# Seven block products for the down-projection, with the activation sums made ahead of it and kept in DRAM

## The chip, the cores and the metric

The kernel runs on one core of a Trainium2 chip. The core has five engines that each follow their own list of instructions: TensorE (PE, matrix products, with a weight load, PEld, ahead of each), VectorE (DVE), ScalarE (ACT), GpSimd (POOL) and SyncE (SP), which here issues all transfers between DRAM and the on-chip memory. Results of TensorE land in eight accumulator banks of 128 x 512 floats. The metric is the device time of one execution in microseconds (us).

## The reference

The reference is a decoder block on 1024 tokens of width 1024, in float32: two attention branches, then a gated MLP with a causal convolution of width 3. Only the MLP matters here. `h` is the modulated norm of the residual stream `x`, `g_f` a row of 1024 numbers worked out from the conditioning vector, D_FF is 2816.

```python
u = h @ w_up                                              # 1024 x 5632
u = conv_b + sum(conv_w[j] * up[:, j:j + s] for j in range(3))
gate, val = u[..., :2816], u[..., 2816:]
x = x + g_f[:, None, :] * ((silu(gate) * val) @ w_down)   # the up stage, then the down stage
return rmsnorm(x, norm_final_g)
```

## The kernel before

Every float32 operand of a product is split into a high and a low part (`hi_act` on ACT writes the high one, `lo_dve` on DVE or `lo_pool` on POOL subtracts it to get the low one), and `mm3` (L95 to L97) issues three matmuls for one: high by high, high by low, low by high. One matmul multiplies a 128 x 128 block by 128 x 512 into one bank.

**The up stage** (`ffn_up`) runs over 22 blocks `j` of 128 hidden columns, tokens on the free axis (1024 of them, two halves of 512). For each block it makes the gate's and the value's columns by seven products instead of eight (a scheme of Strassen and Winograd: sums of blocks are multiplied, and the results are combined): `product` calls of four `mm3` each into the banks x1, x5, x6, x7, combined by ACT copies (`copied`, L1209), seeds (`seed`, L1180: a bank copied into another to go on accumulating there) and DVE subtractions (L1234, L1236). Then come the convolution (`conv`, L1194 on ACT, L1196 on DVE), Silu (L1245) and the product of both (L1247), which is the 128 x 1024 activation block `act`; L1248 stores it to DRAM as `dram_act`.

**The down stage** (`begin_down`, `ffn_down`) is a plain product: for each half of 512 output columns, 22 blocks `k` of the hidden axis by 8 token tiles, each an `mm3`: 2 x 22 x 8 x 3 = 1056 matmuls into the eight banks `mm`. For each block, SP loads `ahp_act` back, ACT and DVE split it (`split_act`: `ahp_ah`/`ahp_al`, in the second half also `an_ah`/`an_al`), and `scaled_rows` loads two blocks of `w_down`, multiplies them on POOL by the row `g_f` (L1124; `gf`) and splits them (`wd_wh`, `wd_wl`). `begin_down` starts this during the last block of the up stage. At the end of the first half DVE adds the eight banks to the residual (L1316), POOL multiplies by the final gain `gl` (L1326). In the second half each token tile is finished by itself: addition (L1333), sum of squares (L1284 on ACT), `rstd` (L102 to L107, small operations), ACT and DVE scale the two halves (L1338, L1339), and SP stores them.

The order on each engine's list is set by a scheduler when the kernel is built, not by the order of the code alone; tiles come from pools in which a new tile waits for the readers of the one that had its place. SP's list is one queue: a transfer that waits holds up all behind it.

## Time and profile before

| what | value |
|---|---|
| median of three runs (lowest, highest) | 1670.74 us (1667.92, 1671.0) |
| the profiled execution: its time, and its span in the trace | 1672.49 us, 1670.4 us |
| instructions | 21073, of them 7702 on PE |
| last matmul of the up stage starts | 1412.36 us |
| first, last matmul of the down stage start | 1418.44 us, 1661.54 us |

Times in the trace count from the span's start. A row of the timeline gives start, duration, engine, line, operation, output tile <- input tiles, shapes, the number of instructions in the row, and in brackets how long the engine was idle ahead of it and what released it. A matmul row's duration (0.39 us) is longer than the distance to the next start (0.23 us), since matmuls are pipelined. Names of tiles begin with their pool: `ps_` is an accumulator bank, `dn_`, `ahp_`, `wd_`, `uw_`, `wr_` are on chip, `dram_` and `in_` in DRAM.

### The profile page before, as it was taken

To read this page: it belongs to the slowest core of one execution; us is meant where nothing else is said; L and a number is where in the kernel's file an instruction comes from. 1 tells how busy PE (TensorE), PEld (TensorE's weight loads), DVE (VectorE), ACT (ScalarE), POOL (GpSimd) and SP (SyncE) were. 2 spreads that over 40 slices of the span, in tenths; PEclk is the share of its full clock that TensorE was granted. 3 is DMA by queue.
4 is the path that set the end of the run, shared out by engine and by line. 5 is a ranking of instruction groups with operands and counts; after the bars stand their busy time and mean duration, and the time that the engine had idled before them with its cause. 6 is when DMAs were issued, how large, how long until landed. Compare 5 with 4: busy or idle time off the path is not lost.

```text
span 1670.4 us, 21073 instructions
## 1 busy us (share of the span) xinstructions
PE 1587.7 (95%) x7702; PEld 1305.3 (78%) x7702; DVE 1048.6 (63%) x1662; ACT 778.2 (47%) x1355; POOL 432.5 (26%) x366
## 2 busy tenths in 40 slices
PE   7899989999979999999998969999999998999997
PEld 3788868888868888887877757888888886788886
DVE  5755666666555656666656698777677774435545
ACT  3424345555444555566433356555555554224324
POOL 1322035665761222202245320000000001324430
PEclk9999999999999999999999979999999999999999
DMA  8435497766564443427435323222222221844443
GB/s 286 139 102 180 166 259 190 211 171 200 148 169 108 113 124 99 123 65 244 138 118 202 125 64 102 84 91 78 88 76 76 81 90 64 291 143 150 164 151 114
DMA packets 172276, 233.33 MB, mean 140 GB/s; under 512 B 10786, under 2 KB 109794, under 8 KB 170830
## 3 DMA queue, kind: packets, MB, share of 16 engines
q1 hardware_dynamic: 172174, 232.01, 44.8%
q8 instruction: 60, 0.98, 0.2%
q14 instruction: 42, 0.34, 0.1%
HBM read 165.90 MB, written 53.48 MB: 131 GB/s over the span
## 4 chain that ended last, share of the span: by engine, by line
PE 46%; DVE 4%; DMA 2%; ACT 1%; issue 1%; POOL 1%; DVEq 0%; ACTq 0%; POOLq 0%; SPq 0%
PE ps_mm L95 11%; PE ps_mm L96 11%; PE ps_mm L97 11%; PE ps_sd L95 4%; PE ps_sd L96 4%; PE ps_sd L97 4%; POOL wr_wr L1124 1%; DMA wr_wr<-in_w_out_dram 1%; DMA wr_wr<-in_w_up_dram 1%; DVE up_u L1196 1%; DMA o_raw<-dram_o 0%; DVE wx_w L85 0%; PE ps_mm L1022 0%; PE psA_pt L97 0%; PE psA_pt L95 0%
## 5 line engine op out<-in xcount | busy, mean ns | idle before, releaser
L1124 POOL TENSOR_TENSOR wr_wr<-wr_wr,ahp_gf 128x512 f32<-128x512 f32 x22 | 33.8, 1560 | 481.9 <-DMA ahp_act<-dram_act 411.6
L95 PE MATMUL psA_fill<-hT_hi,ws_wh 128*128 128x512 f32 x352 | 150.0, 426 | 0.0
L750 ACT ACTIVATE att_p<-psA_s,small_soft 128x128 f32<-128x128 f32 (+7 forms) x128 | 95.0, 742 | 105.0 <-DVE small_soft L744 103.3
L88 POOL TENSOR_TENSOR ws_wl<-wr_wr,ws_wh 128x512 fp32r<-128x512 f32 x62 | 82.6, 1336 | 228.6 <-ACT ws_wh L76 205.7
L97 PE MATMUL psA_fill<-hT_hi,ws_wl 128*128 128x512 f32 x352 | 139.3, 396 | 0.0
L96 PE MATMUL psA_fill<-hT_lo,ws_wh 128*128 128x512 f32 x352 | 139.3, 396 | 0.0
L740 PE MATMUL psA_s<-opn_k,opn_q 96*128 96x256 f32 (+7 forms) x480 | 114.5, 358 | 17.2 <-DMA opn_k<-opn_stg 11.3
L744 DVE TENSOR_REDUCE small_soft<-psA_s 128x1 f32<-128x128 f32 (+7 forms) x128 | 96.1, 752 | 54.5 <-PE psA_s L742 53.9
L1196 DVE SCALAR_TENSOR_TENSOR up_u<-up_u,cw_cw,up_u 128x1023 f32<-128x1023 f32 x88 | 110.9, 1281 | 3.5 <-ACT up_u L1194 2.8
L95 PE MATMUL ps_mm<-wd_wh,ahp_ah 128*128 128x512 f32 x256 | 100.7, 393 | 6.8 <-ACT ahp_ah L76 6.8
L740 PEld LDWEIGHTS psA_s<-opn_k,opn_q 96*128 96x128 f32 (+1 forms) x480 | 81.8, 191 | 26.6 <-issue 16.6
L96 PE MATMUL ps_mm<-wd_wl,ahp_ah 128*128 128x512 f32 x256 | 100.4, 392 | 0.0
L97 PE MATMUL ps_mm<-wd_wh,ahp_al 128*128 128x512 f32 x256 | 99.8, 393 | 0.0
L85 DVE TENSOR_TENSOR ahp_al<-ahp_act,ahp_ah 128x1024 fp32r<-128x1024 f32 x32 | 42.0, 1317 | 88.0 <-ACT ahp_ah L76 88.0
L85 DVE TENSOR_TENSOR att_ptl<-psA_pt,att_pth 128x512 fp32r<-128x512 f32 x96 | 66.1, 688 | 33.9 <-ACT att_pth L76 33.5
L752 DVE TENSOR_SCALAR att_p<-att_p,small_soft 128x128 f32<-128x128 f32 (+7 forms) x128 | 84.1, 657 | 4.1
L769 PE MATMUL psA_pt<-const_ident,att_p 128*128 128x128 f32 x576 | 86.3, 272 | 0.0
L76 ACT ACTIVATE ahp_ah<-ahp_act 128x1024 fp32r<-128x1024 f32 x32 | 33.9, 1061 | 107.5 <-PE ps_mm L96 94.5
L97 PEld LDWEIGHTS psA_fill<-hT_hi,ws_wl 128*128 128x128 f32 x352 | 66.4, 189 | 15.7
L76 ACT ACTIVATE uw_sh<-uw_s 128x1024 fp32r<-128x1024 f32 x44 | 46.8, 1063 | 63.5 <-PE ps_mm L96 28.2
L95 PEld LDWEIGHTS psA_fill<-hT_hi,ws_wh 128*128 128x128 f32 x352 | 67.4, 191 | 9.6
L281 POOL TENSOR_TENSOR att_acc<-att_acc,att_lw 128x512 f32<-128x512 f32 x56 | 73.6, 1314 | 4.3
(411 smaller groups left out, 4518.9 us busy)
## 6 DMA issues: line engine op xcount, KB each, us to landing
wr_wr<-in_w_up_dram SPq DMA_DIRECT2D x46, 512.0 KB
ahp_act<-dram_act SPq DMA_DIRECT2D x44, 512.0 KB
att_lw<-in_w_ada_dram SPq DMA_DIRECT2D x64, 256.0 KB
wr_wr<-in_w_in_dram SPq DMA_DIRECT2D x28, 512.0 KB
dram_act<-up_u SPq DMA_DIRECT2D x22, 512.0 KB
wr_wr<-in_w_down_dram SPq DMA_DIRECT2D x22, 512.0 KB
ada_wada<-in_w_ada_dram SPq DMA_DIRECT2D x16, 512.0 KB
opn_v<-dram_v SPq DMA_DIRECT2D x16, 512.0 KB
```

Of the source, the lines that this page charges most:

```text
L76: self.nc.scalar.activation(out, in_, AF.Copy, scale=scale)
L85: self.nc.vector.tensor_tensor(out=out, in0=in_, in1=f32(hi), op=ALU.subtract)
L88: self.nc.gpsimd.tensor_tensor(out=out, in0=in_, in1=f32(hi), op=ALU.subtract)
L95: mm(ps, lhsT=lh, rhs=rh, start=start, stop=False, skip_group_check=onto)
L96: mm(ps, lhsT=lh, rhs=rl, start=False, stop=False, skip_group_check=onto)
L97: mm(ps, lhsT=ll, rhs=rh, start=False, stop=stop, skip_group_check=onto)
L740: mm(o, lhsT=l, rhs=r[:, keys], start=n_ == 0, stop=diag is None and n_ == len(passes) - 1)
L744: nc.vector.tensor_reduce(out=st[:, 0:1], in_=view(s), axis=AX.X if i < 4 else AX.XY, op=ALU.max, negate=True)
L750: nc.scalar.activation(po, view(s), AF.Exp, bias=st[:, 0:1], accum_out=st[:, 1:2])
L752: nc.vector.tensor_scalar(out=pr, in0=pr, scalar1=st[:, 2:3], scalar2=None, op0=ALU.mult)
L769: nc.tensor.transpose(pt[:, n * 256 + e * P : n * 256 + (e + 1) * P], pr[:, kb * P : (kb + 1) * P], self.ident)
L1196: nc.vector.scalar_tensor_tensor(out=dst[:, back:], in0=u[:, : S - back], scalar=cw[:, tap, jj : jj + 1], in1=dst[:, back:], op0=ALU.mult, ...
```

## The change

The down stage becomes a seven-product scheme too. Its matrices are cut in two by two: the hidden axis into even and odd blocks (11 pairs `m`), the tokens into two halves, the output columns into two halves. The 11 pairs are worked in seven entries, two of one pair, four of two, one of one. The left factors are A11, A12, A22 (parts of the activation) and four sums S1 to S4 of such parts; the right ones B11, B21, B22 (blocks of `w_down`) and sums N1, T2, N3, N4.

- **In the up stage**, `stored` writes the parts of `act` to DRAM, and at each odd block POOL makes the four sums (128 x 512 each), which are stored too: seven left factors of 11 blocks. The seed x7 is gone: the products N3 and N4 accumulate on in x6. The pool of sums holds two tiles of each kind in place of three.
- **`begin_down`** loads and splits the first two entries of A11 and B11 (pairs 10 and 9) during the last block, into places of the up stage's gate operands.
- **`ffn_down`** runs seven products of 11 blocks x 4 token tiles x 3 matmuls = 924 matmuls, and four matmuls that only open the banks Y: 928. For each step (a product and an entry) `operands` loads the left factor (`ring_ar`) and the right one (`ring_br`, or a sum kept on chip), and ACT and DVE split both, one step ahead. The sums N1, T2, N4 of `w_down` are made on DVE in products 0 and 1 and kept. Rows of the residual, `gf` and `gl` are loaded during product 0.
- `w_down` isn't multiplied by `g_f` any more; `result` multiplies the banks by it (L1375, L1379) before the residual is added (L1380). So 22 POOL multiplications per half go, and 40 DVE operations at the ends of products 1, 4, 5 and 6 come (in place of 16 additions).

```diff
@@ ffn_up @@
-            x7 = self.seed(x6, 1.0)
             t = copied(x6)
...
-            self.product(x7, s3, "N3", False)
-            V(out=uv[:, upper], in0=x7, in1=c5, op=ALU.subtract)
+            self.product(x6, s3, "N3", False)
+            V(out=uv[:, upper], in0=x6, in1=c5, op=ALU.subtract)
...
-            self.dma(self.d_act[j], act)
+            self.stored(j, act)
@@ stored @@
+        self.dma(self.place("A12", m), act[:, lower])
+        self.dma(self.place("A22", m), act[:, upper])
+        x, z = (self.upp([P, S], F32, "u", 7) for _ in range(2))
+        G(out=x[:, lower], in0=even[:, upper], in1=act[:, upper], op=ALU.add)
+        G(out=x[:, upper], in0=even[:, lower], in1=even[:, upper], op=ALU.add)
+        G(out=z[:, lower], in0=x[:, lower], in1=even[:, lower], op=ALU.add)
+        G(out=z[:, upper], in0=z[:, lower], in1=act[:, lower], op=ALU.add)
+        for n, y in (("S1", x[:, lower]), ("S3", x[:, upper]), ("S2", z[:, lower]), ("S4", z[:, upper])):
+            self.dma(self.place(n, m), y)
@@ ffn_down @@
-        for k in range(2, NJ):
-            if k % 2 == 0:
-                weights = self.scaled_rows(a["w_down"], k, ns, gain0, self.down_room)
-            held[k % 2] = split_act(self.ahp, k, 2), weights.pop(0)
-            for t in range(NT if k < NJ - 2 else 0):
-                product(acc, t, k, held[k % 2])
...
+        def result(acc, minus, x, ns):
+            if minus is None:
+                y = dn([P, 512], F32, "y", 2)
+                V(out=y, in0=acc, in1=gf[:, ns], op=ALU.mult)
+            else:
+                y = minus
+                V(out=y, in0=acc, in1=minus, op=ALU.subtract)
+                V(out=y, in0=y, in1=gf[:, ns], op=ALU.mult)
+            V(out=x[:, ns], in0=y, in1=x[:, ns], op=ALU.add)
...
+        products = [("A11", "B11", X), ("A12", "B21", X), ("S2", "T2", Y), ("S1", "N1", X), ("S3", "N3", Y), ("S4", "B22", X), ("A22", "N4", Y)]
...
+        for n, (p, i) in enumerate(steps):
+            held = ahead
+            if n + 1 < len(steps):
+                q, k = steps[n + 1]
+                ahead = operands(*products[q][:2], k)
+            matmuls(acc, held, i == 0, i == last, i in (0, last))
+            if (p, i) == (0, 3):
+                self.dma(gf, self.d_row.to_broadcast([P, D]))
+                self.dma(gl, a["norm_final_g"].rearrange("(o d) -> o d", o=1).to_broadcast([P, D]))
+                xs = rows(0)
...
+            elif p == 5:
+                for t in range(4):
+                    result(X[t], saved_t[t], xs[t], sides[1])
+                    finished(t, xs[t], sides[1], squares[t])
```

Three places of the lists, before and after. First SP, where the up stage ends. Before, the last activation block's store (`dram_act_77`) stands behind the loads of the first down blocks, which need earlier blocks alone:

```order
L73 DMA ahp_gf_12393<-dram_row_130 128x512
L73 DMA ahp_act_12409<-dram_act_56_139 128x1024
L73 DMA ahp_act_12415<-dram_act_57_140 128x1024
L73 DMA wr_wr_12587<-in_w_down_dram 128x2x512
L73 DMA dram_act_77_160<-up_u_12419 128x1024
L73 DMA ahp_act_12529<-dram_act_58_141 128x1024
L73 DMA ahp_act_12559<-dram_act_59_142 128x1024
```

Now the last pair's parts and sums (`dram_S_98` is S4) stand ahead of the first loads of the ring, the third entry's operands (`ring_ar_12586`, `ring_br_12588`) among them:

```order
L76 DMA dram_S_77_160<-up_u_12506 128x512
L76 DMA dram_S_84_167<-up_u_12507 128x512
L76 DMA dram_S_98_181<-up_u_12507 128x512
L76 DMA ring_br_12570<-in_w_down_dram 128x512
L76 DMA ring_br_12572<-in_w_down_dram 128x512
L76 DMA ring_br_12575<-in_w_down_dram 128x512
L76 DMA ring_br_12578<-in_w_down_dram 128x512
L76 DMA ring_ar_12586<-dram_A_58_141 128x1024
L76 DMA ring_br_12580<-in_w_down_dram 128x512
L76 DMA ring_br_12583<-in_w_down_dram 128x512
L76 DMA ring_br_12588<-in_w_down_dram 128x2x512
```

What moved: six transfers of `w_down` blocks for the sums and two operand loads now follow the last store, in one queue.

Second, SP in product 0, a new place. `ring_ar_12698` and `ring_br_12700` are the operands of the sixth entry (pairs 1, 2); `ring_br_12650` and `12653` are blocks for the sums of the entry before:

```order
L76 DMA ring_br_12650<-in_w_down_dram 128x2x512
L76 DMA ring_br_12653<-in_w_down_dram 128x2x512
L76 DMA dn_gl_12566<-in_norm_final_g_dram 128x1024
L76 DMA dn_x_12690<-dram_x_48_131 128x1024
L76 DMA dn_x_12692<-dram_x_49_132 128x1024
L76 DMA dn_x_12694<-dram_x_50_133 128x1024
L76 DMA dn_x_12696<-dram_x_51_134 128x1024
L76 DMA ring_ar_12698<-dram_A_61_144 128x1024
L76 DMA ring_br_12700<-in_w_down_dram 128x2x512
```

Nine transfers of 512 KB stand in a row here, of which the first two wait for a place in the ring.

Third, DVE where results are taken. Before, at the end of the first half, one addition per bank:

```order
L85 TENSOR_TENSOR an_al_13203<-ahp_act_13204,an_ah_13202 128x1024
L1316 TENSOR_TENSOR dn_x_1_12439<-ps_mm_1_12449,dn_x_1_12439 128x512
L1316 TENSOR_TENSOR dn_x_2_12440<-ps_mm_2_12450,dn_x_2_12440 128x512
L1316 TENSOR_TENSOR dn_x_3_12441<-ps_mm_3_12451,dn_x_3_12441 128x512
L1316 TENSOR_TENSOR dn_x_4_12442<-ps_mm_4_12452,dn_x_4_12442 128x512
L1316 TENSOR_TENSOR dn_x_5_12443<-ps_mm_5_12453,dn_x_5_12443 128x512
L85 TENSOR_TENSOR an_al_13209<-ahp_act_13210,an_ah_13208 128x1024
```

Now, at the end of product 5, twelve operations for four banks and eight small ones stand between the low parts of the first entry of product 6 (`ring_al_13949`, `ring_bl_13953`) and those of its second (`ring_al_14043`, `ring_bl_14047`). The first rows, and the last:

```order
L88 TENSOR_TENSOR ring_al_13949<-ring_ar_13946,ring_ah_13948 128x512
L88 TENSOR_TENSOR ring_bl_13953<-dn_N_5_12569,ring_bh_13952 128x512
L1378 TENSOR_TENSOR dn_t_13261<-ps_x_1_12522,dn_t_13261 128x512
L1378 TENSOR_TENSOR dn_t_13263<-ps_x_2_12523,dn_t_13263 128x512
L1379 TENSOR_TENSOR dn_t_13261<-dn_t_13261,dn_gf_12565 128x512
L1379 TENSOR_TENSOR dn_t_13263<-dn_t_13263,dn_gf_12565 128x512
L1380 TENSOR_TENSOR dn_x_12690<-dn_t_13261,dn_x_12690 128x512
L1380 TENSOR_TENSOR dn_x_12692<-dn_t_13263,dn_x_12692 128x512
```

```order
L1380 TENSOR_TENSOR dn_x_12696<-dn_t_13267,dn_x_12696 128x512
L108 TENSOR_TENSOR small_rstd_13975<-small_rstd_13975 128x1
L108 TENSOR_TENSOR small_rstd_13993<-small_rstd_13993 128x1
L88 TENSOR_TENSOR ring_al_14043<-ring_ar_14040,ring_ah_14042 128x512
L109 SCALAR_TENSOR_TENSOR small_rstd_13975<-small_rstd_13975 128x1
L109 SCALAR_TENSOR_TENSOR small_rstd_13993<-small_rstd_13993 128x1
L88 TENSOR_TENSOR ring_bl_14047<-dn_N_5_12569,ring_bh_14046 128x512
```

What moved: the split of the next operands follows the whole of the results. At the ends of products 1 and 4 the pattern is the same, with 8 and 12 operations and no small ones between.

## Rows read from the trace of the kernel before

**Rows 1.** The page, first lines: the span, and PE's busy time, share and instructions.

```profile
span 1670.4 us, 21073 instructions
PE 1587.7 (95%) x7702; PEld 1305.3 (78%) x7702; DVE 1048.6 (63%) x1662; ACT 778.2 (47%) x1355; POOL 432.5 (26%) x366
```

**Rows 2.** Windows: PE, PEld, DVE, ACT, POOL busy, granted clock, DMA share, GB/s.

```profile
1010.00:1412.70 402.70, 402.41 (x1750) 328.07 (x1748) 289.54 (x310) 217.38 (x269) 5.02 (x4) 1.00 0.26 83
1412.70:1418.40 5.70, 0.04 (x1) 0.00 (x0) 5.63 (x6) 5.42 (x8) 0.00 (x0) 0.76 0.00 0
1418.40:1662.00 243.60, 242.36 (x1056) 198.98 (x1056) 118.19 (x145) 83.44 (x127) 77.16 (x48) 0.99 0.49 168
1662.00:1670.40 8.40, 0.00 (x0) 0.00 (x0) 3.81 (x15) 2.51 (x7) 0.00 (x0) 0.67 0.44 163
```

**Rows 3.** Waits of PE, 1395 to 1671: total, times, longest.

```profile
PE ps_mm L95 <- ACT ahp_ah L76: 6.8, 2, 5.7
```

**Rows 4.** Timeline of PE: five matmuls of the up and down stages.

```profile
1412.36 0.39 PE L97 MATMUL ps_sd<-t_N,uw_vl 128*128 128x512 f32 x1
1418.44 0.79 PE L95 MATMUL ps_mm<-wd_wh,ahp_ah 128*128 128x512 f32 x1 [5.70 <-ACT ahp_ah L76]
...
1424.03 0.40 PE L95 MATMUL ps_mm<-wd_wh,ahp_ah 128*128 128x512 f32 x1
...
1441.94 0.39 PE L96 MATMUL ps_mm<-wd_wl,ahp_ah 128*128 128x512 f32 x1
...
1661.54 0.39 PE L97 MATMUL ps_mm<-wd_wh,an_al 128*128 128x512 f32 x1
```

**Rows 5.** Windows behind three idle times of PE (3.5, 5.7 and 1.1 us).

```profile
932.10:935.00 2.90, 2.89 (x11) 2.71 (x12) 2.44 (x4) 2.40 (x6) 1.58 (x2) 0.50 0.37 125
1418.40:1422.50 4.10, 4.06 (x9) 2.87 (x10) 4.10 (x6) 1.46 (x2) 0.00 (x0) 0.50 0.66 218
1443.70:1446.00 2.30, 2.30 (x10) 1.92 (x11) 2.23 (x2) 1.06 (x1) 0.78 (x1) 1.00 0.35 121
```

**Rows 6.** Timeline of DVE and POOL around the end of the up stage.

```profile
1404.68 5.02 POOL L1124 TENSOR_TENSOR wr_wr<-wr_wr,ahp_gf 128x512 f32<-128x512 f32 x4 [411.57 <-DMA ahp_act<-dram_act]
1412.18 5.12 DVE L1196 SCALAR_TENSOR_TENSOR up_u<-up_u,cw_cw,up_u 128x1023 f32<-128x1023 f32 x4 [1.38 <-ACT up_u L1194]
1418.42 1.22 DVE L1247 TENSOR_TENSOR up_u<-up_u,up_u 128x1024 f32<-128x1024 f32 x1
```

**Rows 7.** Transfers: a window of the down stage, two loads' issue, the user of the second.

```profile
1430.00:1436.00 6.00, 6.00 (x28) 4.99 (x27) 3.52 (x4) 1.94 (x3) 0.00 (x0) 1.00 1.02 410
1256.97 3.26 SPq L73 DMA_DIRECT2D wr_wr<-in_w_up_dram  x2
1263.84 0.69 DVE L1163 TENSOR_TENSOR uw_s<-wr_wr 128x512 f32<-128x512 f32 x1 [0.29 <-DMA wr_wr<-in_w_up_dram]
```

**Rows 8.** DVE operations back to back; ACT's 128x1024 split, grouped by form.

```profile
993.59 0.68 DVE L1163 TENSOR_TENSOR uw_s<-wr_wr 128x512 f32<-128x512 f32 x1
994.19 0.68 DVE L1164 TENSOR_TENSOR uw_s<-wr_wr,wr_wr 128x512 f32<-128x512 f32 x1
L76 ACT ACTIVATE ahp_ah<-ahp_act 128x1024 fp32r<-128x1024 f32 x31 | 32.9, 1061 | 107.5 <-PE ps_mm L96 94.5 <-PE ps_mm L97 9.5 <-DMA ahp_act<-dram_act 3.4
```

**Rows 9.** Timeline of POOL and DVE while both read on-chip tiles.

```profile
1542.34 10.40 POOL L1326 TENSOR_TENSOR dn_x<-dn_x,dn_gl 128x512 f32<-128x512 f32 x6
1544.63 3.48 DVE L85 TENSOR_TENSOR wd_wl<-wr_wr,wd_wh 128x512 fp32r<-128x512 f32 x2
```

**Rows 10.** Timeline of DVE in the tail: last addition, last small one, last scaling.

```profile
1662.77 0.67 DVE L1333 TENSOR_TENSOR dn_x<-ps_mm,dn_x 128x512 f32<-128x512 f32 x1
1665.80 0.16 DVE L107 SCALAR_TENSOR_TENSOR small_rstd<-small_rstd 128x1 f32<-128x1 f32 x1
1665.99 0.75 DVE L1339 SCALAR_TENSOR_TENSOR dn_x<-dn_x,small_rstd,dn_gl 128x512 f32<-128x512 f32 x1
```

**Rows 11.** A window over one column block of the up stage (columns as in Rows 2).

```profile
1258.10:1277.41 19.31, 19.31 (x85) 15.78 (x84) 14.07 (x16) 10.49 (x14) 0.00 (x0) 1.00 0.26 83
```

More of the change, by code (lines that the diff above doesn't have):

```diff
@@ L1281, in half_squares, with matmuls @@
-        def half_squares(t, n):
+        V, G = nc.vector.tensor_tensor, nc.gpsimd.tensor_tensor
+        X, Y = ([ps([P, 512], F32, f"{n}{i}") for i in range(4)] for n in "xy")
+        sides = [slice(0, 512), slice(512, 1024)]
+        blocks = a["w_down"][0].rearrange("(m e p) n -> e p m n", e=2, p=P)
+        def matmuls(acc, left, first, last, per_tile, tiles=range(4)):
+            ah, al, bh, bl = left
+            n = ah.shape[1]
+            order = [(t, k) for t in tiles for k in range(n)] if per_tile else [(t, k) for k in range(n) for t in tiles]
+            for t, k in order:
+                ts = slice(t * P, (t + 1) * P)
+                self.mm3(acc[t], ah[:, k, ts], al[:, k, ts], bh[:, k, :], bl[:, k, :], first and self.fresh and k == 0, last and self.fresh and k == n - 1, not self.fresh)
@@ new lines, in ffn_down @@
+        self.fresh = True
+        for i, e in enumerate(self.early):
+            matmuls(X, e, i == 0, False, False)
+        ah, al, bh, bl = self.early[0]
+        for y in Y:
+            nc.tensor.matmul(y, lhsT=ah[:, 0, 0:P], rhs=bh[:, 0, :], start=True, stop=True)
+        self.uw1.close()
+        dn = Pool(tc, "dn", "right")
+        ring = Pool(tc, "ring", "right")
+        xs = []
+        gf, gl = dn([P, D], F32, "gf"), dn([P, D], F32, "gl")
+        sums = {n: dn([P, 11, 512], F32, n) for n in ("N1", "T2", "N4")}
@@ L1319, in ffn_down @@
-        ns = slice(512, 1024)
-        acc = [ps([P, 512], F32, f"mm{t}") for t in range(NT)]
-        tail = 4
-        for k in range(0, NJ - tail, 2):
-            held = pair_of(k) if k else ahead
-            if k // 2 < NT:
-                x = x2[k // 2][:, 0:512]
-                nc.gpsimd.tensor_tensor(out=x, in0=x, in1=gl[:, 0:512], op=ALU.mult)
-            for i, t in ((i, t) for t in range(NT) for i in range(2)) if k == 0 else ((i, t) for i in range(2) for t in range(NT)):
-                product(acc, t, k + i, held[i])
@@ new lines, in rows @@
+        def rows(half):
+            out = []
+            for t in range(4 * half, 4 * half + 4):
+                out.append(dn([P, D], F32, "x", 8))
+                self.dma(out[-1], self.d_x1[t])
+            return out
+        products = [("A11", "B11", X), ("A12", "B21", X), ("S2", "T2", Y), ("S1", "N1", X), ("S3", "N3", Y), ("S4", "B22", X), ("A22", "N4", Y)]
+        for i in range(2):
+            right_of("B11", ENTRIES[i])
+        steps = [(p, i) for p in range(7) for i in range(len(ENTRIES)) if (p, i) not in ((0, 0), (0, 1))]
@@ L1342, in ffn_down @@
+        for t in range(4):
+            for held in done:
+                matmuls(Y, held, False, False, True, (t,))
+            result(Y[t], None, xs[4 + t], sides[0])
+            finished(4 + t, xs[4 + t], sides[0], squares[4 + t])
+        ring.close()
         dn.close()
-        an.close()
-        self.ws.close()
-        self.ahp.close()
-        self.uw_t.close()
 _INS = ["x", "c", "positions", "w_ada", "b_ada", "norm_mix_g", "w_in", "q_norm_g", "w_uq", "kv_norm_g", "w_ukv", "b_forget",
```

184 lines of the change are left out of this document (116 added, 68 removed).

## The prediction

> **What bounds the kernel now.** I read the page first: PE is busy 95% of the 1670.4 us span [rows 1]. Then windows by stage: in the last 400 us of the up stage and in the down stage PE is busy throughout (402.41 of 402.70, 242.36 of 243.60 us); only the 5.7 us between them and the 8.4 us at the end are without it [rows 2]. The waits of PE in that stretch say the same: two, 6.8 us in all [rows 3]. So both stages are bound by the count of matmuls. Their price is the distance between starts, not the duration in a row: from 1424.03 to 1441.94 are 79 distances, 0.2267 us each [rows 4].
>
> The down stage before, from the end of the up stage (1412.36 + 0.39 = 1412.75) to the end of its last matmul (1661.54 + 0.23 = 1661.77), takes 249.0 us [rows 4]. Its 1056 matmuls at 0.2267 us are 239.4 us, so it loses 9.6 us already: the wait of 5.7, one of 1.1 [rows 3], some 2.1 at half clock behind the first (9 matmuls take 4.1 us at a granted clock of 0.50, and would take 2.0) [rows 5], and 0.7 in small pieces. A clock of half speed follows the idle times of 3.5 and 5.7 us, and doesn't follow the one of 1.1 us [rows 5]. I charge 2.1 us after an idle time as long as those two.
>
> **The count.** 928 matmuls take the place of 1056: 128 fewer, −29.0 us. With the 9.6 us of old losses gone too, −38.6 us is what the change has to spend on new ones. What can starve PE is that each operand now serves 4 token tiles, not 8: half the time per load.
>
> **Up stage: 0.** Its products are the same. DVE is busy 14.07 of 19.31 us per block, ACT 10.49, POOL 0 [rows 11]; the four POOL sums per pair of blocks (4 x 1.255 = 5.0 us, from the row of 5.02 us for four [rows 6]) run beside DVE, and at worst hold it by the same 5.0 us in 38.6, where it has 10.5 to spare. The seeds that go (one ACT copy per block) weren't waited for. The early entries' transfers and splits lie under the last block. Bounds −2 (a spacing like the down stage's) to +5 (DVE late once per pair for some pairs).
>
> **A, the end of the up stage: +17.2.** The two early entries run without a gap: 28 matmuls (two entries of 12, four openers) x 0.2267 = 6.3 us, to 1419.1. The third entry's loads stand in SP's queue behind the store of S4. That needs the convolution (ends 1417.3 [rows 6]), the product with Silu (1.2 us, without the low parts that stand before it now: 1418.5) and three POOL sums in a chain (3.8 us): 1422.3; with the issues, the loads begin at about 1423.0. Six transfers of 256 KB and two of 512 KB come to 2.6 MB, 6.4 us at the 410 GB/s of the down stage [rows 7]; the fixed part I take from the load whose issue ends at 1260.2 and whose user starts at 1263.8 (3.6 us for 512 KB, of which 1.3 are bytes) [rows 7], 2.3 us: 1431.7 to 1432. Then ACT's split, 1.06 us [rows 8], and DVE's, two spacings of 0.605 (993.59 to 994.19 [rows 8]): 1434.2. PE stands 15.1 us and pays 2.1 for the clock: 17.2. Lower bound 11 (the last store at 1418.5, were the sums off the path), upper 21 (ring places freed late).
>
> **B, product 0, sixth entry: +10.5.** Behind A, three steps of 24 matmuls (5.44 us each, and the 2.1) bring PE to 1452.4. The loads of the sixth entry stand behind two blocks for the sums, `gl` and four rows of the residual: nine transfers of 512 KB. The first waits for a ring place that is free when DVE has made N1 of the fourth entry, about 1445.1. Nine times 1.31 us (512 KB at 400 GB/s) from 1447.1 end at 1458.9; with the splits, 1461.3. PE waits from 1452.4 until the high parts and the first low one are there, 8.4 us, and pays 2.1 for the clock. Lower bound 0 (rows loaded in the shadow of A), upper 14.
>
> A rule of the Trainium skill bears on these loads: the page "DMA: Bandwidth & Descriptors", section Specifications, puts the limit between HBM and one core at about 358 GB/s. The trace disagrees, with 410 GB/s held for 6 us [rows 7]; its price is under the rivals.
>
> **Small steps: +1.2.** 0.4 at the change from product 0 to 1, and 0.8 (0 to 1.5) where a step of 12 matmuls (2.7 us) has a double entry split beside it (2 x 1.06 us on ACT, 4 x 0.605 on DVE [rows 8]): seven products x 0.1.
>
> **C, results on DVE: +19.1.** DVE takes each instruction in its order, so the low parts of the second entry of the next product wait until the results are made. PE can run the first entry's 12 matmuls, and four high-by-high ones of the second: 16 x 0.2267 = 3.6 us behind the end T of a product.
> - Product 5 to 6: the results begin at T − 0.9, when the first entry's low parts are done (their places are free when the entry before has been used, T − 2.7). Twelve operations of 0.605 are 7.3 us, eight small ones of 0.19 (1665.80 to 1665.99 [rows 10]) 1.5, then the two low parts with two small ones between, 1.6: T + 9.4. PE waits 5.8 us; the third entry comes 2.7 late in the same way (four scalings and a dozen small operations stand before its low parts, an estimate from the order and 0.7 and 0.19 us each), and the clock costs 2.1: 10.6.
> - Product 4 to 5: twelve operations and no small ones: T + 7.6, a wait of 4.0; up to 6.3 where POOL's multiplications by `gl` run beside them. With the clock 2.1, or not, I take 6.0.
> - Product 1 to 2: eight operations: T + 5.1, a wait of 1.5; up to 3 with POOL. I take 2.5.
>
> How POOL and DVE slow each other shows in before: six POOL multiplications take 10.40 us, 1.73 each against 1.255 alone, and two DVE splits beside them 3.48 us, 1.74 each against 0.68 [rows 6, 8, 9]. The Trainium skill ("SBUF — State Buffer", section Who interferes with whom) says that a DVE instruction with two on-chip inputs contends with a GpSimd instruction that reads there, and one with an accumulator input doesn't. By that, 8 of the 12 results of a product contend, and product 4 to 5 comes out at its upper end: 8.4 for 6.0, a sum of +14.7.
>
> Lower bound of C 5 (the banks close one after another, so results can begin before T − 0.9, and no clock falls), upper 25 (every split beside POOL at 1.74).
>
> **Tail: +2.9.** Before, from the last matmul's end, 8.6 us pass: 1661.77 to the last DVE end, 1666.74, and 3.66 for the last stores [rows 4, 10]. Now each token tile has two wide operations in place of one, and the last tile's four (result, square on ACT, scale) stand behind those of the tile before: 7.7 us on DVE for 4.8 to 5.0. Bounds +0.6 (one operation) to +4.
>
> **Sum.** −38.6 + 17.2 + 10.5 + 1.2 + 19.1 + 2.9 = +12.3 us. The profiled execution took 1672.49 us, 2.1 over its span and 1.75 over the median; the span comes to 1682.7, and the median of 1670.74 to 1683.0. That is the prediction.
>
> **Rivals.**
> 1. The results are covered: DVE gets the next operands' low parts done in time at the three product changes, and C goes to nothing. Time 1683.0 − 19.1 = 1663.9, faster than before. For it: DVE is busy only 118.19 of the 243.60 us of the down stage [rows 2]. Against it: the order, in which the low parts stand behind the results; DVE has the time, but not then. It decides from the point where A, B, C and the small steps come to less than 35.7 us.
> 2. The residual's rows are hidden: B's loads come in the 15 us in which PE waits in A, or the queue of the ring is further ahead than I worked out, and B costs nothing. Time 1672.5. For it: DMA moves 168 GB/s on average in the stage [rows 2], far below 410. Against it: one queue and four ring places, of which the blocks for the sums take three per entry.
> 3. Transfers bind product 0. A step with a double entry moves four times 512 KB in 5.44 us, 386 GB/s, 6% below the 410 of the down stage [rows 7]; new transfers write and read at the same time at its start. Were 10% less to be had (369), a step would last 5.68 us, 0.24 more for each of four, A's and B's transfers 0.7 and 1.3 more: 1686. By the page's 358 it would be 1687. Against it, the row of 410 over 6 us.
> 4. POOL's sums hold DVE in the up stage, at 22 blocks 0.2 us each: 1688. Against it the 5 us per block in which DVE is idle [rows 11].
> 5. The change doesn't do what it says: not possible on the count, since the list of PE has 128 matmuls less.
>
> **How the numbers follow.** Forecast (1676 to 1691) 0.52, rival 1 0.18 (1660 to 1667), rival 2 0.15 (1668 to 1676), rival 3 0.05, rival 4 0.07, the rest 0.03. What a measurement of this kernel can tell from no change is about 0.2%, 3.3 us: same is 1667.4 to 1674.1. From rival 1 nearly all of 0.18 is faster; rival 2 splits into 0.01 faster, 0.12 same, 0.02 slower; the forecast and rivals 3 and 4 are slower. Faster 0.19, same 0.13, slower 0.68. The range of 8 in 10 leaves out the lower part of rival 1 and the highest cases: 1664 to 1695; the likeliest case's own is 1676 to 1691.
>
> **What would show it.** In the profile after, PE's waits from 1412 on are the test: one of about 15 us at 1419 released by the split of a ring tile, one of about 8 us in product 0, five to nine at the ends of products 4 and 5, released by DVE, each followed by a window at half clock; 928 matmuls at 0.227 us; a tail of 11.5 us. The up stage ends at 1412 to 1413. If PE's waits together come to less than 30 us I was wrong on the side of rival 1; if A's wait is short, wrong on the store of S4; if B has none, on the rows of the residual.

## The result: 1.3% slower

The changed kernel takes 1691.36 us (median of four runs, 1687.38 to 1695.55); the kernel before, on the same chips, 1670.87 (1667.92 to 1671.64). The ratio is 1.0126, 95% interval 1.0098 to 1.0155. Forecast was 1683.0 us in a range of 1664 to 1695; the median is 3.6 us under the range's upper end and 0.4 over the likeliest case's own range (1676 to 1691). The profiled execution took 1692.81 us, its span is 1691.0 us, 20.6 over the one before.

The page's first lines, to be laid beside [rows 1]: 128 matmuls fewer and 13 us less of busy PE in a longer span.

```profile
span 1691.0 us, 21093 instructions
...
PE 1574.5 (93%) x7574; PEld 1291.4 (76%) x7574; DVE 1083.8 (64%) x1722; ACT 783.3 (46%) x1353; POOL 420.8 (25%) x366
```

PE's waits from 1395 us on, where the kernel before had two of 6.8 us in all [rows 3]. Five of the six are the waits the prediction named: two for loads, three for low parts from DVE at the changes of products 1 to 2, 4 to 5 and 5 to 6. The sixth, also for a low part, is 1.4 us at the change of products 3 to 4.

```profile
PE ps_x L98 <- ACT ring_bh L79: 25.0, 2, 16.7
PE ps_y L99 <- DVE ring_bl L88: 11.1, 3, 5.0
PE ps_x L99 <- DVE ring_bl L88: 6.3, 1, 6.3
```

Windows (PE, PEld, DVE, ACT, POOL, granted clock, DMA share, GB/s): the up stage; the early entries; the first wait; what follows it; the stretches behind the waits in product 0 and at the ends of products 1, 4 and 5; the tail. Each of the five long waits is followed by a stretch at half clock, as the two in [rows 5].

```profile
1000.00:1414.00 414.00, 412.16 (x1787) 336.12 (x1786) 297.70 (x319) 213.15 (x256) 56.33 (x41) 1.00 0.31 100
...
1414.20:1419.60 5.40, 5.40 (x26) 4.46 (x25) 5.22 (x5) 2.91 (x3) 0.00 (x0) 1.00 0.00 0
1419.60:1437.30 17.70, 1.03 (x6) 0.53 (x4) 4.41 (x7) 2.11 (x2) 3.79 (x3) 0.66 0.80 276
1437.30:1442.30 5.00, 4.96 (x11) 3.47 (x12) 4.77 (x4) 1.06 (x1) 0.00 (x0) 0.50 0.92 326
...
1464.80:1469.70 4.90, 4.84 (x11) 3.34 (x12) 4.79 (x5) 1.26 (x2) 0.00 (x0) 0.50 0.85 302
1514.50:1517.60 3.10, 3.07 (x8) 2.46 (x9) 3.10 (x3) 0.00 (x0) 0.00 (x0) 0.52 0.64 192
1614.10:1620.00 5.90, 5.83 (x14) 4.58 (x15) 4.71 (x5) 2.00 (x2) 1.15 (x1) 0.51 0.83 251
1651.70:1657.40 5.70, 5.70 (x13) 4.42 (x14) 5.70 (x20) 3.95 (x7) 0.00 (x0) 0.50 0.90 294
1681.10:1691.00 9.90, 0.14 (x1) 0.00 (x0) 5.73 (x23) 4.25 (x11) 0.00 (x0) 0.68 0.57 212
```

**A table by stage** carries all that follows. From PE's timeline I take the start of each matmul of the down stage; all 928 are there in each trace. A stage's loss is the time from its first start to the next stage's, less its matmuls at 0.2267 us each. "Early" is the early entries and the wait behind them (the clock it costs falls into product 0). p0 to p6 are the products; the results of a product are made, and waited for, in the next one. All in us; the sums are of the losses before rounding.

| kernel | up stage ends | early | p0 | p1 | p2 | p3 | p4 | p5 | p6 | sum | span |
|---|---|---|---|---|---|---|---|---|---|---|---|
| changed kernel | 1414.1 | 16.8 | 13.8 | 0.2 | 6.6 | 0.2 | 1.7 | 9.2 | 7.9 | 56.6 | 1691.0 |
| e1 stores on ACT's queue | 1412.0 | 15.1 | 12.1 | 0.4 | 8.1 | 0.2 | 1.0 | 8.7 | 7.7 | 53.3 | 1686.1 |
| e2 rows in product 1 | 1411.7 | 16.7 | 4.8 | 2.0 | 6.6 | 0.2 | 1.0 | 8.3 | 7.4 | 47.1 | 1679.0 |
| e3 results later | 1416.7 | 17.2 | 13.4 | 0.4 | 2.3 | 0.2 | 1.0 | 2.0 | 0.3 | 37.0 | 1673.9 |
| e5 loads for sums later | 1410.0 | 10.3 | 20.0 | 0.2 | 6.8 | 0.2 | 1.2 | 8.0 | 7.2 | 54.0 | 1684.4 |
| e6 rows of 4 KB | 1411.5 | 16.6 | 10.1 | 1.2 | 8.0 | 0.2 | 20.6 | 9.0 | 7.8 | 73.6 | 1705.3 |
| e7 no gain on POOL | 1411.5 | 16.7 | 14.5 | 0.3 | 1.8 | 0.2 | 1.0 | 7.0 | 8.1 | 49.6 | 1681.4 |
| e8 all together | 1410.7 | 11.9 | 9.3 | 4.5 | 1.6 | 0.2 | 16.3 | 2.4 | 0.3 | 46.5 | 1677.8 |
| e9 sums in two products | 1415.0 | 10.4 | 5.9 | 2.5 | 3.8 | 0.2 | 1.1 | 4.2 | 0.3 | 28.4 | 1663.7 |
| e10 four early entries | 1415.0 | 4.0 | 10.2 | 4.7 | 2.8 | 0.2 | 1.2 | 2.0 | 0.3 | 25.4 | 1660.6 |
| e11 stores and late sums | 1412.9 | 7.2 | 23.3 | 0.2 | 6.7 | 0.2 | 1.0 | 8.0 | 7.3 | 54.0 | 1687.8 |
| e12 early and ACT queue | 1412.2 | 4.4 | 10.5 | 3.8 | 2.8 | 0.2 | 1.2 | 2.0 | 0.3 | 25.3 | 1657.6 |

Each row is one trace. The up stage ends between 1410.0 and 1416.7 with the same code up to there in nearly all, so some 6 us of scatter come from earlier stages, and single spans are compared by the table's losses. A single time can't tell anything within the changed kernel's own 8 us either: e4, e5, e6, e7 and e11 have one run each and are read from their traces.

### The profile page after: what moved, and what is told of

Read it like the earlier page. It is cut to its first block, busy times and chain, and to the rows that moved or that the text cites. A ratio compares the mean times of both kernels' runs of the same rounds, so it can differ in the third digit from the quotient of the medians.

```text
span 1691.0 us, 21093 instructions
## 1 busy us (share of the span) xinstructions
PE 1574.5 (93%) x7574; PEld 1291.4 (76%) x7574; DVE 1083.8 (64%) x1722; ACT 783.3 (46%) x1353; POOL 420.8 (25%) x366
## 3 DMA queue, kind: packets, MB, share of 16 engines
q1 hardware_dynamic: 185614, 246.96, 47.1%
## 4 chain that ended last, share of the span: by engine, by line
PE 43%; DVE 5%; DMA 3%; issue 2%; POOL 1%; ACT 1%; SPq 0%; DVEq 0%; POOLq 0%; ACTq 0%
PE ps_mm L98 6%; PE ps_mm L100 6%; PE ps_mm L99 6%; PE ps_sd L98 4%; PE ps_sd L99 4%; PE ps_sd L100 4%; PE ps_x L99 2%; PE ps_x L98 2%; PE ps_x L100 2%; PE ps_y L99 2%; PE ps_y L100 2%; DMA ring_br<-in_w_down_dram 2%; PE ps_y L98 1%; POOL wr_wr L1127 1%; DMA wr_wr<-in_w_out_dram 1%
## 5 line engine op out<-in xcount | busy, mean ns | idle before, releaser
L79 ACT ACTIVATE ring_ah<-ring_ar 128x1024 fp32r<-128x1024 f32 (+1 forms) x47 | 41.6, 885 | 134.9 <-PE ps_x L99 57.6
L88 DVE TENSOR_TENSOR ring_al<-ring_ar,ring_ah 128x1024 fp32r<-128x1024 f32 (+1 forms) x47 | 49.5, 1053 | 80.5 <-ACT ring_ah L79 80.4
L98 PE MATMUL ps_x<-ring_bh,ring_ah 128*128 128x512 f32 x168 | 66.2, 405 | 25.0 <-ACT ring_bh L79 25.0
L88 DVE TENSOR_TENSOR att_ptl<-psA_pt,att_pth 128x512 fp32r<-128x512 f32 x96 | 66.1, 688 | 34.4 <-ACT att_pth L79 33.9
L88 DVE TENSOR_TENSOR uw_gl<-wr_wr,uw_gh 128x1024 fp32r<-128x1024 f32 x24 | 29.4, 1223 | 82.4 <-ACT uw_gh L79 82.4
L99 PE MATMUL ps_x<-ring_bl,ring_ah 128*128 128x512 f32 x168 | 68.9, 410 | 6.4 <-DVE ring_bl L88 6.3
L99 PEld LDWEIGHTS psA_fill<-hT_lo,ws_wh 128*128 128x128 f32 x352 | 66.9, 190 | 9.8
```

The costliest lines, as they stand in the source:

```text
L79: self.nc.scalar.activation(out, in_, AF.Copy, scale=scale)
L88: self.nc.vector.tensor_tensor(out=out, in0=in_, in1=f32(hi), op=ALU.subtract)
L98: mm(ps, lhsT=lh, rhs=rh, start=start, stop=False, skip_group_check=onto)
L99: mm(ps, lhsT=lh, rhs=rl, start=False, stop=False, skip_group_check=onto)
```

## The experiments

**e1, the last stores from ACT's queue.** In `stored`:

```
+        store = self.nc.scalar.dma_start if j == NJ - 1 else self.dma
-            self.dma(self.place(n, m), y)
+            store(self.place(n, m), y)
```

> One edit: the last pair's six stores of A12, A22 and the four sums go out from ACT's queue, so SP's loads of the ring no longer stand behind the store of S4. Theory (the queue): the first ring load is issued when the last product of the up stage is done, about 1420, for 1424.6 in the changed kernel, and PE's wait at the end of the up stage falls from 16.7 us to 11 to 13; nothing else moves; time 4 to 5 us less than the changed kernel. Rival (transfers): the wait is set by the bytes of the eight transfers ahead of the operand, which moved at only 300 to 330 GB/s there; stores and loads then run at the same time and slow each other, and the wait falls by less than 2 us.

1689.31 us, ratio to before 1.0109 (1.0054 to 1.0163). The loads began 5.6 us after the up stage's end (1417.6), not 10.5 (1424.6), but the wait only fell from 16.7 to 14.9. SP's queue in the changed kernel, where the third store is S4:

```profile
1420.19 0.80 SPq L76 DMA_DIRECT2D dram_A<-up_u  x2
1421.53 3.00 SPq L76 DMA_DIRECT2D dram_S<-up_u  x3
1424.62 1.82 SPq L76 DMA_DIRECT2D ring_br<-in_w_down_dram  x4
1426.49 0.43 SPq L76 DMA_DIRECT2D ring_ar<-dram_A  x1
```

and in e1:

```profile
1417.61 4.32 SPq L76 DMA_DIRECT2D ring_br<-in_w_down_dram  x4
1422.51 0.80 SPq L76 DMA_DIRECT2D ring_ar<-dram_A  x2
1423.86 2.07 SPq L76 DMA_DIRECT2D ring_br<-in_w_down_dram  x3
```

So the wait fell by less than 2 us, as the rival said. The rival put it down to bytes; the trace shows another thing beside them. By its account the last of the first four loads waited 2.7 us until a store issued by ACT had landed; why a load waits for it isn't shown. SP's waits in e1, from 1412 us to 1466, in total, times, longest:

```profile
SPq L76 <- DMA dram_A<-up_u: 3.2, 2, 2.7
```

Early and p0 together lost 27.2 us for 30.6, so part of the head start was kept in product 0.

**e5, the loads for the sums behind the third entry's operands**, the other half of that question.

```
-        for i in range(2):
-            right_of("B11", ENTRIES[i])
         ...
         ahead = operands(*products[0][:2], 2)
+        for i in range(2):
+            right_of("B11", ENTRIES[i])
```

> One edit: the third entry's operands are loaded ahead of the six w_down blocks for the sums of the first two entries, not behind them; all else, the bytes too, stays. Theory (bytes in one queue): PE's wait at the end of the up stage falls from 16.7 us by the 1.6 MB that no longer stand ahead, at the 300 GB/s of that stretch 4 to 6 us, to 11 to 13; but product 0 still has to load the same bytes, so part comes back as a longer wait or new ones before the entries behind, and the loss of PE from the end of the up stage to the end of product 0 (30.3 us in the changed kernel, half clock included) falls by 0 to 3 us only. Rival (latency of the first load): the wait falls by 4 to 6 us and the whole loss by as much.

1686.14 us (one run). The wait fell to 10.2 us, and the rest of product 0 lost 20.0 for 13.8: early and p0 together 30.3 after 30.6. So, with the same transfers in another order, the waits only moved to another place of product 0.

**e11, both of these.**

```
+        store = self.nc.scalar.dma_start if j == NJ - 1 else self.dma
...
         ahead = operands(*products[0][:2], 2)
+        for i in range(2):
+            right_of("B11", ENTRIES[i])
```

> The edits of the first run (last pair's stores from ACT's queue) and of the fifth (third entry's operands ahead of the loads for the sums) together. Alone, the first took 1.7 us from the loss at the end of the up stage, the second 6.5. Theory (each hides the other: with 1.6 MB ahead of the operands the bytes decide, without them the store does): together they take more than the sum, 16.8 to between 4 and 7 us, since the operands' loads start some 5 us earlier and have nothing ahead. Rival (they add): 8 to 9 us are left. Either way the loss of early entries and product 0 together stays at 27 to 31 us, being set by bytes.

1689.62 us (one run). 7.2 us are left of "early", 9.6 less than in the changed kernel where the two edits alone took 1.7 and 6.5: a little more than their sum, so each hides a little of the other, less than I expected. Early and p0 stay at 30.5; what e1 won there is not seen again, and SP waits for the same store, here 4.2 us at one load.

**e2, the residual's rows in product 1**, one transfer per step.

```
-            if (p, i) == (0, 3):
-                self.dma(gf, ...); self.dma(gl, ...); xs = rows(0)
+            if (p, i) == (1, 0): self.dma(gf, ...)
+            if (p, i) == (1, 1): self.dma(gl, ...)
+            if p == 1 and 2 <= i <= 5: xs.append(...); self.dma(xs[-1], self.d_x1[i - 2])
```

> One edit: gf, gl and the first four rows of the residual are loaded one per step in product 1, not in a row in product 0. Theory (the queue in product 0): PE's wait of 8.35 us before the sixth entry goes to under 1 us with the half clock behind it (2.4 us), and no wait comes up in product 1, whose steps need 1 MB in 5.4 us; time 9 to 11 us less than the changed kernel. Rival (ring places): the sixth entry waits for the places that the blocks of the sums hold, and 4 us or more of the wait stay. Second rival (moved, not gone): the same transfers starve a step of product 1, and a wait of 3 us or more shows there.

1687.74 us, ratio 1.0093 (1.0073 to 1.0114). The 8.35 us wait became 0.5, p0 lost 9.0 less, p1 1.8 more. The term B was what it was said to be, with 7.2 us to be won net in the trace. That trace is of the fastest of the five runs (1680.80; the others 1685.65 to 1688.11): by the medians only 3.6 us are won, not the 9 to 11 expected, within what the two kernels scatter. In the changed kernel the nine transfers show at once: DMA moves 409 GB/s while PE has nothing (1458.00 to 1462.40).

```profile
1458.00:1462.40 4.40, 0.00 (x0) 0.00 (x0) 0.00 (x0) 0.04 (x1) 0.00 (x0) 0.66 1.02 409
```

**e3, the results one tile per step**, behind the splits of that step's operands.

```
+            if later and i > 0:
+                later.pop(0)()
...
-                for x, acc in zip(xs, X):
-                    result(acc, None, x, sides[0])
-                squares = [first_half(x, sides[0]) for x in xs]
+                later += [lambda t=t: taken(t, X[t], None, xs[t], sides[0]) for t in range(4)]
```

(and so for products 4 and 5; `taken` is `result` and `first_half` of one tile)

> One edit: the results of products 1, 4 and 5 are written one token tile per step of the next product, behind the splits of that step's operands, not in one piece at the product's end. Theory (DVE's order): the three waits of PE for low parts (5.0, 6.3 and 4.7 us) go to under 1 us each, with the half clock behind them (1.4, 2.6 and 3.1 us); time 20 to 24 us less than the changed kernel, at or just under the kernel before. Rival (DVE's work): the same operations only come later, POOL's multiplications by gl still run beside the splits, and waits of 3 us or more in sum come up in steps two to five of products 2, 5 and 6; time 10 to 14 us less.

1675.43 us, ratio 1.0013 (0.9995 to 1.0031): no longer to be told from the kernel before, 15.9 us less than the changed kernel by the medians. p2, p5 and p6 lose 4.7 us for 23.8, and PE's waits for low parts are down to three of 0.7 to 2.0 us:

```profile
PE ps_y L99 <- DVE ring_bl L88: 2.7, 2, 2.0
PE ps_x L99 <- DVE ring_bl L88: 1.6, 1, 1.6
```

The three waits were DVE's order, with the half clock behind them; DVE's work was not the reason, since it stayed the same (164.1 us in the down stage in both).

**e7, no multiplication by the final gain on POOL** in `first_half`: the kernel leaves the gain out of one half of each output row.

```
-            G(out=x[:, ns], in0=x[:, ns], in1=gl[:, ns], op=ALU.mult)
```

> One edit, and it leaves out part of the computation: POOL's eight multiplications of a finished half by the final gain are not made, so one half of each output row lacks the gain. Theory (DVE and POOL get in each other's way): the splits behind the results go back from 1.75 us to 0.6, PE's wait at product 1 to 2 falls from 5.0 us to 1.0 to 2.2 and that at product 4 to 5 from 6.3 to 3.7 to 4.7; that at product 5 to 6, where POOL does nothing, stays at 4.7. Rival (ACT): the sums of squares on ACT hold the splits, and the two waits move by less than 1 us.

1683.15 us (one run). The waits at products 1 to 2 and 4 to 5 went from 5.0 and 6.3 us to 1.5 and 3.9, that at 5 to 6 stayed at 4.7. DVE in the changed kernel, from the results of product 1 on (L1375, L1380), then the low parts (L88):

```profile
1507.25 1.28 DVE L1375 TENSOR_TENSOR dn_y<-ps_x,dn_gf 128x512 f32<-128x512 f32 x2
1508.45 2.69 DVE L1380 TENSOR_TENSOR dn_x<-dn_y,dn_x 128x512 f32<-128x512 f32 x2
1511.06 1.75 DVE L88 TENSOR_TENSOR ring_al<-ring_ar,ring_ah 128x512 fp32r<-128x512 f32 x1
1512.73 1.74 DVE L88 TENSOR_TENSOR ring_bl<-dn_T,ring_bh 128x512 fp32r<-128x512 f32 x1
```

with POOL's four beside it:

```profile
1507.62 6.31 POOL L1384 TENSOR_TENSOR dn_x<-dn_x,dn_gl 128x512 f32<-128x512 f32 x4 [83.44 <-ACT dn_sqb L1368]
```

and in e7:

```profile
1505.32 1.28 DVE L1375 TENSOR_TENSOR dn_y<-ps_x,dn_gf 128x512 f32<-128x512 f32 x2
1506.52 1.28 DVE L1380 TENSOR_TENSOR dn_x<-dn_y,dn_x 128x512 f32<-128x512 f32 x2
1507.72 0.68 DVE L88 TENSOR_TENSOR ring_al<-ring_ar,ring_ah 128x512 fp32r<-128x512 f32 x1
1508.32 0.68 DVE L88 TENSOR_TENSOR ring_bl<-dn_T,ring_bh 128x512 fp32r<-128x512 f32 x1
```

The last splits before PE goes on take 1.75 us beside POOL and 0.68 without; two additions with both inputs on chip (L1380) take 2.69 and 1.28. The results that read an accumulator (L1375, 1.28 for two) take the same in both, which agrees with the Trainium skill ("SBUF — State Buffer", section Who interferes with whom).

**e4, fillers in the first wait.**

```
-        for y in Y:
+        for y in Y * 20:
```

> One edit: 80 opening matmuls in place of 4, on operands that are there, so that PE has work of 17 us in the wait at the end of the up stage (the banks Y that they write are opened anew by the last four, so the result is the same). Theory (clock): matmuls after the wait start 0.23 us apart, not 0.43, and the granted clock stays at 1.00; the 2.5 us lost behind the wait are won, the third entry still begins at about 1437 to 1438. Rival (operands): the 0.43 us spacing comes from operands that arrive late, and stays. The single time can't tell, being within the kernel's own scatter; the profile decides.

1698.87 us (one run). As a test of the clock it failed: with PE busy until 1435.4 the scheduler put `gf`, `gl` and seven rows of the residual ahead of the ring, whose loads began at 1428.9, and PE then waited 13.1 us all the same, with half clock behind it (0.50 from 1448.5 to 1453.0). It shows B once more from the other side: with the rows loaded early, product 0 lost 6.6 us, not 13.8.

**e6, B11 and B12 in one transfer of 4 KB rows.**

```
-            w = ring([P, 2, 512], F32, "br", 4)[:, : len(e), :]
+            w = ring([P, 2, 512], F32, "br", 2)[:, : len(e), :]
...
+        def wide(e):
+            w = ring([P, 2, 1024], F32, "bw", 2)[:, : len(e), :]
+            self.dma(w, blocks[0][:, e[0] : e[-1] + 1, :])
+            return w[:, :, 0:512], w[:, :, 512:1024]
...
-                v = raw(e, 0, 1)
+                w, v = wide(e)
```

> One edit: B11 and B12 come in one transfer with rows of 4 KB, not in two with rows of 2 KB; same bytes, same sums. Theory (row length): the 300 to 330 GB/s of the stretch behind the up stage, where rows of 2 KB are loaded, against 410 where rows of 4 KB are, is due to the rows; with two thirds of the w_down bytes of product 0 in long rows the rate goes to 350 to 400, PE's wait at the end of the up stage falls by 1.5 to 3 us, and the loss up to the end of product 0 by 4 us or more. Rival (order of loads): the rate of that stretch is set by waits for ring places and for the stores, stays at 300 to 330, and the loss moves by less than 2 us.

1707.11 us (one run). The wait stayed (16.5), early and p0 together lost 26.7 for 30.6. The rates did rise, from the second window on. The changed kernel:

```profile
1424.60:1431.00 6.40, 0.00 (x0) 0.00 (x0) 1.39 (x2) 0.00 (x0) 0.00 (x0) 0.55 0.89 298
1431.00:1437.00 6.00, 0.00 (x0) 0.00 (x0) 2.43 (x3) 1.88 (x2) 0.00 (x0) 0.50 0.90 305
1440.00:1448.00 8.00, 8.00 (x32) 6.52 (x31) 4.88 (x5) 2.12 (x2) 0.00 (x0) 0.85 0.97 349
```

and e6:

```profile
1422.00:1428.00 6.00, 0.00 (x0) 0.00 (x0) 1.38 (x2) 0.00 (x0) 0.00 (x0) 0.54 0.91 305
1428.00:1434.00 6.00, 0.00 (x0) 0.00 (x0) 3.28 (x4) 1.73 (x2) 0.00 (x0) 0.50 1.03 403
1437.00:1445.00 8.00, 8.00 (x31) 6.43 (x31) 6.24 (x6) 2.70 (x4) 0.00 (x0) 0.84 1.03 401
```

Half for the theory, then: long rows go with 400 GB/s, but the first operand brings 1 MB where 0.5 did, so it comes no sooner. What made the kernel slower is another thing: product 4, which loads two blocks per step, lost 20.6 us with two places for blocks in place of four; e8, with two, loses 16.3 there, and e9, with four again, 1.1.

**e8, all together** but the stores: e3 and e5 as above, the 4 KB rows and so two ring places, the residual's rows in product 2, T2 made in product 1 from blocks loaded with B21.

```
+            w, v = wide(e, int(name[1]) - 1)
             if name == "B11":
...
                 V(out=sums["N1"][:, ms, :], in0=w, in1=v, op=ALU.subtract)
...
+            if name == "B21":
                 V(out=sums["T2"][:, ms, :], in0=v, in1=sums["N1"][:, ms, :], op=ALU.add)
...
+            if p == 2 and i < 4:
+                xs.append(dn([P, D], F32, "x", 8))
+                self.dma(xs[-1], self.d_x1[i])
```

> Several edits that the runs before speak for: results one tile per step behind the splits; residual rows and gains loaded at the end of product 1 and in product 2; the third entry's operands first; blocks of w_down in rows of 4 KB (B11 with B12 in product 0, B21 with B22 in product 1), so that T2 is made in product 1 and B11 is loaded once. Product 0 loads 30% less. Theory (all of the loss is waits for loads and for DVE's order): PE loses 9 to 12 us at the end of the up stage with 2.3 behind it, under 3 us in the rest of product 0, under 5 in all the changes of products; in sum 16 to 22 us for 56; time 1650 to 1657 us, faster than the kernel before by 0.8 to 1.3%. Rival (a new bound): product 1, which now loads 1.5 MB per step, or DVE, which makes two sums per step there, waits 5 us or more, and the time is no better than the kernel before.

1679.76 us, ratio 1.0057 (1.0038 to 1.0077): slower than the kernel before by 0.6%, where 0.8 to 1.3% faster was expected. p4 lost 16.3, the price of the two places that I had not reckoned with; p0 9.3, where under 3 was expected, and p1 4.5. e9 and e10 take the loss in p4 back.

**e9, the sums in two products**, four ring places and the 2 KB rows of the changed kernel kept, e3, e5 and the rows in product 2 as in e8.

```
             if name == "B11":
                 v = raw(e, 0, 1)
                 V(out=sums["N1"][:, ms, :], in0=w, in1=v, op=ALU.subtract)
-                v = raw(e, 1, 1)
-                V(out=sums["T2"][:, ms, :], in0=v, in1=sums["N1"][:, ms, :], op=ALU.add)
             if name == "B21":
+                v = raw(e, 1, 1)
+                V(out=sums["T2"][:, ms, :], in0=v, in1=sums["N1"][:, ms, :], op=ALU.add)
```

> Edits against the changed kernel: results one tile per step behind the splits; B22 loaded for T2 and N4 in product 1, not in product 0 (2.9 MB less there); residual rows and gains loaded at the end of product 1 and in products 2 and 3; the third entry's operands first; the four ring places for blocks of w_down kept, rows of 2 KB. Theory (product 0 is bound by its bytes, product 4 in the run of all together by its two ring places): PE loses 10 to 12 us at the end of the up stage, 2 to 6 in the rest of product 0, under 3 in product 1, under 2 in product 4, 5 at most in products 2, 5 and 6; 18 to 24 us in sum for 56.4; time 1652 to 1659 us, 0.7 to 1.1% under the kernel before. Rival (bytes only move): product 1 then loads 1.5 MB per step in 5.4 us and loses 5 us or more, and the time is not under the kernel before.

1662.53 us, ratio 0.9948 (0.9934 to 0.9963): faster than the kernel before. Early 10.4, p0 5.9, p1 2.5 as expected; p2, p5 and p6 lose 8.3 for an expected 5 at most, so the sum is 28.4 for 18 to 24 and the time is 3.5 us over the expected range's upper end.

**e10, e9 with two more early entries**, two loads of 512 KB each, split into places of `ew`; the ring is allocated ahead of the other tiles, and the loads for the sums of the four early entries follow the first operands, two at a time.

```
+        ew = self.ew = Pool(self.tc, "ew", "left")
+        for i in range(4):
+            if i > 1:
...
-        dn = Pool(tc, "dn", "right")
         ring = Pool(tc, "ring", "right")
+        dn = Pool(tc, "dn", "right")
```

> As the kernel before it in this call, and two double entries more (pairs 7, 8 and 5, 6 of A11 and B11) loaded and split during the last block of the up stage, into the places of the up stage's right operands; the ring's places lie where the up stage frees memory first. Theory (the wait at the end of the up stage lasts until the first operands behind the last store are there, about 11 us whatever PE has to do till then): 48 more matmuls, 10.9 us, fill the wait, which falls to 0 to 5 us; product 0 has 2 MB less to load and loses 0 to 5 us in its rest; in sum 8 to 16 us for 56.4; time 1644 to 1651 us, 1.2 to 1.6% under the kernel before. Rival (DVE and ACT are late): the extra splits hold up the last convolution and the last store, or come late themselves, PE waits within the early entries by 4 us or more, and the gain against the other kernel of this call is under 4 us.

1661.12 us, ratio 0.9929 (0.9910 to 0.9948), the fastest of all by its median; against e9 no clear difference, where 8 us were expected. The wait shrank to 2.7 us, but DVE's splits of the extra entries stood between the convolution's steps, the store of S4 went out at 1429.6, and p0 and p1 lost 14.9 us: the gain over e9 is under 4 us, as the rival said.

**e12, e10 with the stores on ACT's queue.**

```
+        store = self.nc.scalar.dma_start if j == NJ - 1 else self.dma
```

> As the kernel with four early entries, with the last pair's stores from ACT's queue. There the loads of the ring started at 1430.1 behind the store of S4, 15 us after the up stage's end, and PE lost 4.0 us before and 10.2 in product 0. Theory (the store, held up by POOL's sums and the extra splits, still stands ahead of the loads): the loads start about 5 us earlier, the loss before product 0's ring entries goes to 0 to 1.5 us and that in its rest to 4 to 8; time 4 to 8 us less, 1653 to 1657. Rival (the loads then wait for ring places and for the stores' own bytes): loss and time change by less than 2 us.

1661.99 us, ratio 0.9938 (0.9919 to 0.9958). Early and p0 lost 14.9 us for 14.3: nothing won, as the rival said, but the edit did not do what it was meant to. The loads of the ring still began 14.6 us after the up stage's end, for 15.0 in e10, with no store ahead of them in SP's queue: by the trace's account the first one waited for POOL's last sum. Its row, and SP's wait (1412 to 1436):

```profile
1426.77 0.32 SPq L76 DMA_DIRECT2D ring_ar<-dram_A  x1
SPq L76 <- POOL up_u L1274: 3.1, 1, 3.1
```

So e12 says nothing on bytes.

## Why the prediction was right, and where its sizes were off

Right in direction and in every place of loss in the down stage; the sum was +12.3, the trace has +20.6 (−38.6, then 56.6 lost in the down stage, 1.4 at the up stage's end and 1.3 in the tail, each rounded). The place of each wait was forecast from the order of the lists, the sizes missed by 8. All but the tail's and one part of C's missed the same way, so that the time still lies in the range is owed to the range's width more than to the sizes; one of the four runs (1695.55) lies outside.

- **The count**, −29.0: 928 matmuls, 0.227 us apart at full clock (median). Right.
- **Up stage**, 0: it ended 1.4 us later, within the scatter of the table, but it has a loss that is the change's own and was put at nothing. Once per execution N4, accumulating on in x6, waits for DVE's subtraction that reads that bank: 1.7 to 2.1 us in all thirteen traces after the change. In nine of them, the changed kernel's too, a stretch of half clock follows, which costs some 1.5 us more:

```profile
1062.17 0.50 PE L98 MATMUL ps_sd<-t_N,uw_vh 128*128 128x512 f32 x1 [1.84 <-DVE up_u L1236]
1063.50:1066.90 3.40, 3.40 (x10) 2.62 (x9) 3.40 (x5) 1.95 (x3) 0.00 (x0) 0.50 0.00 0
```

  Before there were 0.9 us in two waits of the stage, 0.6 for a seed's copy and 0.3 for a subtraction, and no half clock behind them. I had only counted the copies that went, and said that they weren't waited for. From 1012 us to the stage's end, at 0.2267 us a matmul, the changed kernel loses 9.2 us and the kernel before 6.1.
- **A**, 17.2: measured 19.3 (16.8 and 2.5 of half clock). The loads began 10.5 us after the up stage's end, where 10.25 was worked out; they then took 12.7 us to the split, not 11.2, at 298 to 305 GB/s in place of the 410 of [rows 7]. And the name was wrong in part: I charged the store of S4, but without the store ahead only 1.7 us of the wait are won (e1), without the sums' bytes 6.5 (e5), and product 0 gives the latter back (with both, e11, early and p0 lose 30.5 us for 30.6; with the stores moved alone, e1, 27.2).
- **B**, 10.5: measured 10.9 (8.5 and 2.4). Right, shown by e2.
- **Small steps**, 1.2: 2.2 us (p1, p3, p4), 1.4 of them one wait at the change of products 3 to 4.
- **C**, 19.1: measured 23.8. Product 1 to 2 is the term that was mis-sized: 2.5 forecast, 6.6 measured. Its own bounds were 1.5 without POOL and 3 with it; e7 measures 1.5 without and 5.0 with, plus a half clock (1.4) that I had not charged there. I had let POOL slow the results, but it slowed the splits behind them more (by 2.1 us, the results by 1.4). Product 4 to 5: 6.0, measured 9.2; the wait is 3.9 without POOL, where 4.0 was worked out. Product 5 to 6: 10.6, measured 7.9; the wait was 4.7 for 5.8, and the third entry wasn't late.
- **Tail**, +2.9: measured +1.3 (9.9 us for 8.6). DVE needs 6.2 us from the end of the last matmul (1681.08) to the end of its last scaling, not 7.7; the last stores take 3.7 as before.

```profile
1686.52 0.75 DVE L1394 SCALAR_TENSOR_TENSOR dn_x<-dn_x,small_rstd,dn_gl 128x512 f32<-128x512 f32 x1
```

Of the rivals, the first (results covered) is what e3 makes true by hand: it needs another order, and gives about the time of the kernel before. The second (B hidden) is e2. That transfers bind product 0, rival 3, which I gave 0.05, is what e2 and e9 speak for, where fewer bytes lose less (early and p0 21.6 and 16.4 us for 30.6), with e5 and e11, where the same bytes in another order lose the same. From the first load to the start of product 1 they move at 320 GB/s; a limit of 358 isn't the reason, since 409 is reached with the rows of the residual.

```profile
1424.60:1475.60 51.00, 29.88 (x109) 23.09 (x110) 26.44 (x27) 12.40 (x16) 0.00 (x0) 0.73 0.90 320
SPq L76 <- DVE dn_N L1339: 16.2, 6, 4.8
```

How much of that is the rate of the transfers and how much is waiting isn't settled. The second row is SP between 1420 and 1476: six waits, 16.2 us in all, for DVE's N1 sums, the readers of the ring's places, and no run gave the ring more places. Nor is it settled why the 2 KB rows of `w_down` go slower: e6 raised the rate with longer rows and also changed how many transfers are in flight.

## What to carry to other kernels

A scheme that saves matmuls on a stage bound by them can shorten the time that each load and each split has; here it halved it, since an operand serves 4 token tiles, not 8. Work out bytes per step against the rate, stage by stage, before counting matmuls. Read the lists in order at each change of accumulators: results of several operations that stand ahead of the next operands cost their length and a stretch of half clock, and to emit them one per step behind the splits took 19.1 of 23.8 us here. Moving a load within product 0 won nothing (e5, e11); moving it out of product 0 did (e2, e9).
